# Rebuilding the first ten microseconds of a two-layer encoder kernel on one Trainium2 core

## The chip, the cores and the metric

The kernel runs on one core of a Trainium2 chip. The metric is the device time of one execution in microseconds (us). The kernel before takes 529.43 us, the median of 3 runs (529.13 to 529.46). A profile of one more execution is read as well; that execution took 529.6 us, and its span, from the first to the last instruction, is 527.8 us.

## What is computed

The reference is two layers of a hybrid encoder over 256 tokens of width 1024 in float32. Layer 0 is one shared input projection whose columns feed a Mamba-2 scan (`z`, `xbc`, `dt`) and stick-breaking attention (`q`, `k`, `v`), an output projection, a normalisation, and a mixture of 16 gated experts. Layer 1 has two other kinds of attention and another mixture. Only the very start of layer 0 matters here:

```python
h = x @ w_in
z, xbc, dt_raw, q, k, v = _split(h, [...])        # dt_raw: 16 columns, one per head
...
dt = jax.nn.softplus((dt_raw + dt_bias).astype(f32))
```

## The kernel before

The input is held transposed, `xT`: 128 partitions, 8 chunks of 256 tokens. A product in nearly full float32 precision is made of three cheaper ones: each operand is split into a rounded `hi` part and the remainder `lo`, and `hi*hi`, `hi*lo` and `lo*hi` are accumulated (`mm3_stationary`, L235 to L243). ScalarE writes a `hi` (L231, and L320 for the input), VectorE subtracts to get `lo` (L232, and L321 for the input).

The input projection is cut into 32 strips of 128 columns. Two strips come in one 1 MB weight tile `w`, so strip 0 is the first half of the first tile and strip 1 its second half. A strip costs TensorE 24 products of 128x256 (8 chunks times three parts). `presplit(i)` (L326) emits the split of strip i, two strips ahead of its products. The split parts live in a pool of 3 buffers (`hp`, L101), so the split of strip 3 takes the buffer that strip 0 leaves. Weight tiles come through a ring of 19 buffers that `fill` (L164) keeps full from SyncE's queue (SP in the profile); once the buffers are taken, a load is issued when TensorE or VectorE has finished with an old one.

Each engine works through its own list in the order in which the Python code emits it (a manual schedule); a waiting instruction holds up what is behind it on its engine. The opening, `mixer0` (L306) up to the strip loop (L541), emits in this order:

- SyncE: the 64 KB weights of `dt` (`wdt`, L312), the input in four quarters (L314), then in `load_constants` the first weight tile in two halves, the second tile, the small parameters `pp`, the third tile, the constants `cc` and `cm`, and the rest of the ring.
- ScalarE: the load of an activation table (L248), four pieces of `xh` (L320), the `hi` of strips 0 and 1, a copy of dt's product out of PSUM (L344), the `hi` of strip 2, and so on.
- VectorE: four pieces of `xl` (L321), then the `lo` of strips 0, 1, 2.
- TensorE: dt's product (L340) as plain float32 products, 8 chunks of 128x16 weights by 256 columns, each two records in the trace; then strip 0, strip 1, and so on. Ahead of strip 5, two small transposes (L357) turn dt's product to tokens by heads.

The kernel already has a product of the form that the change gives to dt: the router's logits (L883) put chunk c on the column group c % 4 of TensorE, and one product with the constant `fold` (L893) adds the four groups up.

Of the kernel before, what the change touches and what calls it, by code (L numbers as in the profile page):

```python
# [9 lines left out]
F32 = mybir.dt.float32  # L10
F32R = mybir.dt.float32r
BF16 = mybir.dt.bfloat16
# [81 lines left out]
class Builder:  # L94
# [69 lines left out]
    def fill(self, n=1000, parts=1):  # L164
        while n and self.loaded < len(self.seq) and self.free > self.keep:
            if self.loaded in self.elsewhere:
                self.loaded += 1
                continue
            src = self.seq[self.loaded]
            rows, n_el = src.shape  # L170
            w = self.wp.tile([128, 2048], F32, tag="w", name="w")
            for i in range(parts):
                cs = slice(n_el * i // parts, n_el * (i + 1) // parts)
                self.nc.sync.dma_start(w[:rows, cs], src[:, cs])
            self.ring[self.loaded] = w
            self.loaded += 1
            self.free -= 1
            n -= 1
# [56 lines left out]
    def mm3_stationary(self, ps, hi, lo, xh, xl, n=8):  # L235

        mm = self.nc.tensor.matmul
        for c in range(n):
            mm(ps, hi[:, c, :], xh[:, c, :], start=(c == 0), stop=False)  # L239
        for c in range(n):  # L240
            mm(ps, hi[:, c, :], xl[:, c, :], start=False, stop=False)  # L241
        for c in range(n):
            mm(ps, lo[:, c, :], xh[:, c, :], start=False, stop=(c == n - 1))  # L243


    def load_constants(self):
        nc = self.nc
        nc.scalar.preload_act_table_set(EXP_LN)  # L248
        self.fill(1, 2)
        self.fill(1)  # L250
        self.pp = self.cp.tile([128, NPP], F32, name="pp")
        nc.sync.dma_start(self.pp, self.a["pp"])
        self.fill(1)
        self.cc = self.cp.tile([128, NC0], F32, name="cc")
        nc.sync.dma_start(self.cc, self.a["cc"][:, :NC0])
# [50 lines left out]
    def mixer0(self):  # L306
# [4 lines left out]
        wdt = self.T([128, 8, 16], name="wdt")  # L311
        nc.sync.dma_start(wdt.rearrange("p c n -> p (c n)"), self.a["wdt"])  # L312
        for i in range(4):
            nc.sync.dma_start(xT[:, i * 512:(i + 1) * 512], self.a["xT"][:, i * 512:(i + 1) * 512])  # L314
        self.load_constants()
        xh = self.G([128, 8, 256], F32R, "xh")
        xl = self.G([128, 8, 256], F32R, "xl")
        xT3 = xT.rearrange("p (c t) -> p c t", c=8)
        for i in range(4):
            sc.activation(xh[:, 2 * i:2 * i + 2], xT3[:, 2 * i:2 * i + 2], AF.Copy)  # L320
            v.tensor_sub(xl[:, 2 * i:2 * i + 2], xT3[:, 2 * i:2 * i + 2], xh[:, 2 * i:2 * i + 2].bitcast(F32))  # L321
# [21 lines left out]
        dts = [self.T([128, 512], name="dts")]  # L343
        sc.activation(dts[0][:16, :256], dtp[:16, :256], AF.Copy)  # L344
# [8 lines left out]
        def steps():  # L353
            dtt = self.B("dtt")
            d = dts.pop()
            for t in range(2):
                pe.transpose(dtt[:, 16 * t:16 * t + 16], d[:16, 128 * t:128 * t + 128], self.ident[:16, :16])  # L357
            tmp = self.T([128, 128], name="sptmp")
            v.tensor_add(dt, dtt[:, :32].rearrange("p (t h) -> p t h", t=2),
# [181 lines left out]
        for i in range(32):  # L541
# [1187 lines left out]
def lay_out(inputs):  # L1729
    f = np.ascontiguousarray  # L1730
    x = inputs["x"][0]
    o = {}
# [42 lines left out]
    o["wdt"] = f(dt.reshape(8, 128, 16).transpose(1, 0, 2).reshape(128, 128))  # L1775
# [31 lines left out]
```

## Time and profile before

| | |
|---|---|
| time, median of 3 | 529.43 us (529.13 to 529.46) |
| profiled execution, its span | 529.6 us, 527.8 us |
| TensorE busy | 499.3 us, 95% of the span |
| VectorE, ScalarE, GpSimd busy | 299.5, 247.8, 116.6 us |
| moved from and to memory | 142.37 MB, 270 GB/s over the span |
| first product of TensorE | 4.55 us after the span's start |
| first product of strip 0, of strip 2 | 11.03 us, 16.83 us |

The engines are PE (TensorE; PEld is its weight load, which overlaps products), ACT (ScalarE), DVE (VectorE), POOL (GpSimd) and SP (SyncE); SPq and ACTq are their queues for issuing transfers. All times in rows are counted from the start of the span. A row of the timeline can merge several instructions, and its second number then is the time from the first one's start to the last one's end; a product's end is modelled, so the distance between starts tells more than a length.

### The profile page before, as it was taken

Reading aid. Unit: us, or ns where it says so; the run is one execution under the profiler, and the core shown is the slowest. Engines: PE = TensorE matmul, PEld = TensorE weight load, DVE = VectorE, ACT = ScalarE, POOL = GpSimd, SP = SyncE. Lnnn points to the kernel's source line nnn. Section 1 sums busy time; section 2 is a strip of 40 time slices with the busy share of each in tenths; the row PEclk is TensorE's granted clock in tenths of the full one; section 3 lists DMA queues with packets and bytes.
Section 4 is the critical chain, followed back from the end, with each engine's and each line's share of the span. In section 5 each row is a group of like instructions: output and inputs, shape, how many; then the busy total and the mean of one; then the engine's idle time right before and its main releaser. Section 6 shows DMA issues by size and latency. Waiting matters only on the chain. (4 is left out here: it accounts for less than half of the span.)

```text
span 527.8 us, 9789 instructions
## 1 busy us (share of the span) xinstructions
PE 499.3 (95%) x3844; PEld 321.1 (61%) x3844; DVE 299.5 (57%) x664; ACT 247.8 (47%) x519; POOL 116.6 (22%) x168
## 2 busy tenths in 40 slices
PE   6999999989999999999999998899999999999990
PEld 3999998878677543433323698787777343533320
DVE  3776647678877763160206774788667741512047
ACT  4786565559674442250214683465644431512031
POOL 0073124350300001150002068442000002700204
PEclk9999999999999999999999999999999999999996
DMA  8999942006267969999979923061468799999602
GB/s 281 420 420 417 380 160 81 1 1 240 80 230 266 417 240 395 422 407 418 418 286 418 384 95 138 22 251 69 161 238 329 294 407 409 424 402 425 264 1 79
DMA packets 21178, 142.37 MB, mean 270 GB/s; under 512 B 2372, under 2 KB 2628, under 8 KB 4740
## 3 DMA queue, kind: packets, MB, share of 16 engines
q1 hardware_dynamic: 20024, 135.67, 64.1%
q0 software_dynamic: 816, 5.51, 2.9%
q8 instruction: 32, 0.52, 0.4%
q10 hardware_dynamic: 288, 0.52, 0.3%
q14 instruction: 18, 0.15, 0.1%
HBM read 140.64 MB, written 1.05 MB: 268 GB/s over the span
## 5 line engine op out<-in xcount | busy, mean ns | idle before, releaser
L1022 PE MATMUL gu<-w,XT 128*32 128x512 f32 x960 | 107.0, 593 | 0.0
L232 DVE TENSOR_TENSOR pair<-w,pair 128x1024 fp32r<-128x1024 f32 x50 | 62.7, 1257 | 22.1 <-ACT pair L231 21.8
L1022 PEld LDWEIGHTS gu<-w,XT 128*32 128x32 f32 x960 | 29.7, 110 | 65.4 <-issue 61.5
L231 ACT ACTIVATE pair<-w 128x1024 fp32r<-128x1024 f32 x57 | 60.2, 1059 | 9.1 <-PE ps L243 3.7
L1052 PE MATMUL dn<-w,hT 128*32 128x512 f32 x512 | 59.5, 596 | 0.9 <-ACT hT L1041 0.9
L1032 DVE TENSOR_TENSOR hd<-sg,gu 128x256 f32<-128x256 f32 x16 | 6.7, 421 | 83.5 <-ACT sg L1030 83.4
L779 POOL PARTITION_BROADCAST w<-w x16 | 11.2, 798 | 163.7 <-DMA w<-in_ln_dram 75.9
L1071 DVE SCALAR_TENSOR_TENSOR pair<-dn,ws,pair 128x512 fp32r<-128x512 f32 x30 | 22.5, 749 | 36.4 <-ACT pair L1065 34.4
L239 PE MATMUL ps<-xh,pair 128*128 128x256 f32 x288 | 42.1, 288 | 0.0
L241 PE MATMUL ps<-xl,pair 128*128 128x256 f32 x288 | 39.9, 280 | 0.0
L243 PE MATMUL ps<-xh,pair 128*128 128x256 f32 x288 | 39.8, 280 | 0.0
L1065 ACT ACTIVATE pair<-dn,ws 128x512 fp32r<-128x512 f32 x30 | 20.6, 688 | 37.5 <-PE dn L1052 29.9
L239 PEld LDWEIGHTS ps<-xh,pair 128*128 128x128 f32 x288 | 36.4, 189 | 1.5 <-issue 1.0
L243 PEld LDWEIGHTS ps<-xh,pair 128*128 128x128 f32 x288 | 36.6, 188 | 0.0
L241 PEld LDWEIGHTS ps<-xl,pair 128*128 128x128 f32 x288 | 36.5, 188 | 0.0
L1030 ACT ACTIVATE sg<-gu 128x256 f32<-128x256 f32 x16 | 6.1, 382 | 62.5 <-PE gu L1022 62.5
L1052 PEld LDWEIGHTS dn<-w,hT 128*32 128x32 f32 x512 | 14.4, 109 | 30.7 <-issue 25.7
L992 ACT ACTIVATE XT<-gp,pp 128x256 f32<-128x256 f32 x36 | 17.5, 564 | 19.2 <-PE gp L985 19.2
L232 POOL TENSOR_TENSOR pair<-w,pair 128x1024 fp32r<-128x1024 f32 x7 | 17.0, 2424 | 37.5 <-ACT pair L231 37.5
L1544 ACT ACTIVATE pw<-z,sm 128x128 f32<-128x128 f32 (+1 forms) x32 | 13.0, 420 | 23.4 <-DVE sm L1541 17.0
L394 DVE SCALAR_TENSOR_TENSOR cy<-ps,pp,cy 128x255 f32<-128x255 f32 (+2 forms) x36 | 17.3, 480 | 5.6 <-ACT cy L391 4.8
L302 PE MATMUL vp<-pair,xh 128*128 128x256 f32 x128 | 19.9, 288 | 0.4 <-POOL pair L232 0.4
(371 smaller groups left out, 968.9 us busy)
## 6 DMA issues: line engine op xcount, KB each, us to landing
w<-in_wgu_dram SPq DMA_DIRECT2D x60, 1024.0 KB, 9.8
w<-in_wd_dram SPq DMA_DIRECT2D x32, 1024.0 KB, 11.8
w<-in_w_dram SPq DMA_DIRECT2D x15, 1024.0 KB, 18.1
w<-in_wout_dram SPq DMA_DIRECT2D x10, 1024.0 KB, 18.6
wh<-in_wgu_dram POOLq DMA_DIRECT2D x4, 1024.0 KB, 7.2
w<-in_wfox_dram SPq DMA_DIRECT2D x4, 1024.0 KB, 16.0
w<-in_wfv_dram SPq DMA_DIRECT2D x2, 1024.0 KB, 4.9
w<-in_wab_dram SPq DMA_DIRECT2D x2, 848.0 KB, 17.5
```

The costliest lines, as they stand in the source:

```text
L231: self.nc.scalar.activation(vh, src, AF.Copy)
L232: (self.nc.gpsimd if pool else self.nc.vector).tensor_tensor(vl, src, vh.bitcast(F32), op=OP.subtract)
L239: mm(ps, hi[:, c, :], xh[:, c, :], start=(c == 0), stop=False)
L241: mm(ps, hi[:, c, :], xl[:, c, :], start=False, stop=False)
L243: mm(ps, lo[:, c, :], xh[:, c, :], start=False, stop=(c == n - 1))
L302: mm(o, xx[:, 4 * k + c, 128 * t:128 * t + 128], ww[:, c, :], start=(k == 0 and n == 0), stop=(k == 1 and n == 11))
L394: v.scalar_tensor_tensor(y[:, k:], ps[:, :256 - k], self.pp[:, i:i + 1], y[:, k:], op0=OP.mult, op1=OP.add)
L992: sc.activation(xt[:, c, :], b[:, i], AF.Identity, bias=bb, scale=g)
L1022: pe.matmul(gu[t][32 * e:32 * e + 32, :], XT[t][:, c, o:o + 32], w[:, e, :], start=(c == 0), stop=(c == 7))
L1052: pe.matmul(b[32 * e:32 * e + 32, :], ht[:, k, 32 * e:32 * e + 32], w[:, e, :], start=(k == 0), stop=(k == 1))
L1065: sc.activation(y, dn[t, s], AF.Copy, scale=WS[t][:, q:q + 1])
L1071: v.scalar_tensor_tensor(yl, b, WS[t][:, q:q + 1], yh.bitcast(F32), op0=OP.mult, op1=OP.subtract)
```

## The change

The opening is rebuilt in these parts. The first weight tile is issued from ScalarE's queue, ahead of the table load, in the same two halves; `wdt` is issued from GpSimd's queue and is padded to 32 columns a chunk (128 KB); the input comes in two halves instead of four quarters. VectorE clears a 128x512 bf16 tile, and TensorE multiplies it by itself 8 times into a PSUM buffer that nobody reads. The last two of the four pieces of `xh` move from ScalarE to VectorE. dt's product puts chunk c on column group c % 4, the copy out of PSUM takes 128 partitions instead of 16, and two products with `fold` take the place of the two transposes. Last, strips 0 and 1 both get their `hi*hi` and `hi*lo` products first, and their `lo*hi` products after.

```diff
     def load_constants(self):
         nc = self.nc
+        self.fill(1, 2, nc.scalar)
         nc.scalar.preload_act_table_set(EXP_LN)
-        self.fill(1, 2)
         self.fill(1)
...
-        wdt = self.T([128, 8, 16], name="wdt")
-        nc.sync.dma_start(wdt.rearrange("p c n -> p (c n)"), self.a["wdt"])
-        for i in range(4):
-            nc.sync.dma_start(xT[:, i * 512:(i + 1) * 512], self.a["xT"][:, i * 512:(i + 1) * 512])
+        wdt = self.T([128, 8, 32], name="wdt")
+        nc.gpsimd.dma_start(wdt.rearrange("p c n -> p (c n)"), self.a["wdt"])
+        for cs in (slice(0, 1024), slice(1024, 2048)):
+            nc.sync.dma_start(xT[:, cs], self.a["xT"][:, cs])
         self.load_constants()
+
+        idle = self.T([128, 512], BF16, name="idle")
+        v.memset(idle, 0.0)
+        wu = self.B("wu")
+        for i in range(8):
+            pe.matmul(wu, idle[:, :128], idle, start=True, stop=True)
+        del wu
...
         for i in range(4):
-            sc.activation(xh[:, 2 * i:2 * i + 2], xT3[:, 2 * i:2 * i + 2], AF.Copy)
-            v.tensor_sub(xl[:, 2 * i:2 * i + 2], xT3[:, 2 * i:2 * i + 2], xh[:, 2 * i:2 * i + 2].bitcast(F32))
+            cs = slice(2 * i, 2 * i + 2)
+            if i < 2:
+                sc.activation(xh[:, cs], xT3[:, cs], AF.Copy)
+            else:
+                v.tensor_copy(xh[:, cs], xT3[:, cs])
+            v.tensor_sub(xl[:, cs], xT3[:, cs], xh[:, cs].bitcast(F32))
...
         for c in range(8):
-            pe.matmul(dtp[:16, :256], wdt[:, c, :], xT3[:, c, :], start=(c == 0), stop=(c == 7))
+            r = slice(32 * (c % 4), 32 * (c % 4) + 32)
+            pe.matmul(dtp[r, :256], wdt[:, c, :], xT3[:, c, :], start=(c < 4), stop=(c >= 4))
...
-        sc.activation(dts[0][:16, :256], dtp[:16, :256], AF.Copy)
+        sc.activation(dts[0], dtp[:, :256], AF.Copy)
...
-                pe.transpose(dtt[:, 16 * t:16 * t + 16], d[:16, 128 * t:128 * t + 128], self.ident[:16, :16])
+                pe.matmul(dtt[:, 32 * t:32 * t + 32], d[:, 128 * t:128 * t + 128], self.cv("fold"), start=True, stop=True)
...
+            if i == 0:
+
+                ps2 = [self.A("ps")[:, :256] for _ in range(2)]
+                for k in range(2):
+                    self.mm3_stationary(ps2[k], *pieces[k], xh, xl, parts=(0, 1))
             presplit(i + 2)
             hi, lo = pieces.pop(i)
             ps = None
-            if i >= 28:
+            if i < 2:
+                ps = ps2[i]
+                self.mm3_stationary(ps, hi, lo, xh, xl, parts=(2,))
+            elif i >= 28:
```

In `mm3_stationary`, `parts` chooses among the three loops (0 is `hi*hi`, 1 is `hi*lo`, 2 is `lo*hi`); in `fill`, `queue` names the engine that issues.

## Rows read from the trace of the kernel before

**Rows 1.** The page's first part: busy time, share of the span, instructions of each engine.
```profile
PE 499.3 (95%) x3844; PEld 321.1 (61%) x3844; DVE 299.5 (57%) x664; ACT 247.8 (47%) x519; POOL 116.6 (22%) x168
```

**Rows 2.** PE's waits, whole span: us in total, times, longest us.
```profile
PE dtp L340 <- DMA xT<-in_xT_dram: 4.5, 1, 4.5
PE hT L1462 <- POOL qk L1312: 1.8, 1, 1.8
```

**Rows 3.** Windows: PE, PEld, DVE, ACT, POOL busy (instructions), PEclk, DMA share, GB/s.
```profile
11.00:60.00 49.00, 49.00 (x411) 48.70 (x411) 36.05 (x53) 35.17 (x54) 14.54 (x39) 1.00 1.01 420
60.00:120.00 60.00, 58.34 (x488) 52.82 (x487) 39.15 (x65) 36.21 (x79) 22.86 (x15) 1.00 0.24 88
```

**Rows 4.** Timeline of the opening: start us, us, engine, line, out<-in, count [idle before <-releaser].
```profile
0.81 1.28 ACT L248 ACT_TABLE_LOAD   x1 [0.81 <-PEq L1796]
0.82 0.39 SPq L312 DMA_DIRECT2D wdt<-in_wdt_dram  x1
1.26 1.84 SPq L314 DMA_DIRECT2D xT<-in_xT_dram  x4
3.15 1.38 SPq L174 DMA_DIRECT2D w<-in_w_dram  x3
4.44 0.63 ACT L320 ACTIVATE xh<-xT 128x512 fp32r<-128x512 f32 x1 [2.35 <-DMA xT<-in_xT_dram]
6.68 1.26 ACT L320 ACTIVATE xh<-xT 128x512 fp32r<-128x512 f32 x2 [0.56 <-DMA xT<-in_xT_dram]
9.74 1.06 ACT L231 ACTIVATE pair<-w 128x1024 fp32r<-128x1024 f32 x1 [1.81 <-DMA w<-in_w_dram]
11.02 1.06 ACT L231 ACTIVATE pair<-w 128x1024 fp32r<-128x1024 f32 x1 [0.22 <-DMA w<-in_w_dram]
```

**Rows 5.** Timeline of PE alone, 0 to 17 us.
```profile
4.55 6.55 PE L340 MATMUL dtp<-xT,wdt 128*16 128x256 f32 x16 [4.55 <-DMA xT<-in_xT_dram]
11.03 1.22 PE L239 MATMUL ps<-xh,pair 128*128 128x256 f32 x8
13.98 1.11 PE L239 MATMUL ps<-xh,pair 128*128 128x256 f32 x8
16.83 0.40 PE L239 MATMUL ps<-xh,pair 128*128 128x256 f32 x2
```

**Rows 6.** Windows of the opening, columns as in Rows 3.
```profile
2.00:4.00 2.00, 0.00 (x0) 0.00 (x0) 0.00 (x0) 0.09 (x1) 0.00 (x0) 1.00 0.76 226
4.00:5.00 1.00, 0.45 (x2) 0.20 (x3) 0.00 (x0) 0.56 (x1) 0.00 (x0) 1.00 0.78 238
7.00:8.00 1.00, 1.00 (x4) 0.37 (x3) 0.66 (x2) 0.94 (x2) 0.00 (x0) 1.00 0.95 295
10.00:11.00 1.00, 1.00 (x4) 0.27 (x2) 0.17 (x1) 0.80 (x1) 0.00 (x0) 1.00 1.00 422
```

**Rows 7.** Products of 256 columns, three lines (L239 to 18 us): duration ns min/median/max.
```profile
L340 PE MATMUL dtp<-xT,wdt x16: 379/631/631, 4.5 to 10.7; 128*16 128x256 f32 x16
L428 PE MATMUL cbp<-bc x4: 377/379/381, 34.3 to 38.0; 128*128 128x256 f32 x4
L239 PE MATMUL ps<-xh,pair x24: 277/281/392, 11.0 to 17.7; 128*128 128x256 f32 x24
```

**Rows 8.** Groups by form: busy us, mean ns of one.
```profile
L507 DVE CAST sph<-spz 128x384 fp32r<-128x384 f32 x8 | 2.8, 352 | 0.0
L321 DVE TENSOR_TENSOR xl<-xT,xh 128x512 fp32r<-128x512 f32 x4 | 2.7, 692 | 6.0 <-ACT xh L320 6.0
L232 DVE TENSOR_TENSOR pair<-w,pair 128x1024 fp32r<-128x1024 f32 x50 | 62.7, 1257 | 22.1 <-ACT pair L231 21.8
```

**Rows 9.** Issues from POOL and ACT: duration ns min/median/max, and us to landing of L840's.
```profile
L840 POOL DMA_DIRECT2D wrg<-in_wr_dram x2: 740/801/862, 43.3 to 330.9; - x2
DMA to landing us min/median/max: 2.6/4.6/6.5
...
L799 ACTq DMA_DIRECT2D out_dram<-xres x2: 339/366/394, 522.9 to 524.4; - x2
```

**Rows 10.** Timeline of PE around the router's products in column groups.
```profile
165.90 0.39 PE L684 MATMUL acc<-pair,yh 128*128 128x512 f32 x1
166.22 0.65 PE L883 MATMUL rp<-xT,wrg 128*32 128x128 f32 x16
166.80 0.50 PE L682 MATMUL acc<-pair,yh 128*128 128x512 f32 x1
167.37 0.39 PE L684 MATMUL acc<-pair,yh 128*128 128x512 f32 x1
167.60 0.30 PE L893 MATMUL lg<-cc,rl 128*128 128x32 f32 x2
167.74 0.48 PE L682 MATMUL acc<-pair,yh 128*128 128x512 f32 x1
```

**Rows 11.** Timeline of PE around dt's two transposes.
```profile
25.47 0.29 PE L357 MATMUL dtt<-cc,dts 16*128 16x16 f32 x2
25.69 0.50 PE L239 MATMUL ps<-xh,pair 128*128 128x256 f32 x2
```

**Rows 12.** Timeline of PE, its last products.
```profile
514.14 1.12 PE L1088 MATMUL acc<-yl,PT 128*128 128x512 f32 x2
```

**Rows 13.** Windows after them, columns as in Rows 3.
```profile
517.00:519.00 2.00, 0.00 (x0) 0.00 (x0) 1.93 (x5) 0.66 (x3) 1.92 (x2) 1.00 0.00 0
519.00:520.00 1.00, 0.00 (x0) 0.00 (x0) 0.96 (x2) 0.00 (x0) 1.00 (x2) 0.55 0.00 0
```

More of the change, by code (lines that the diff above doesn't have):

```diff
@@ L162, in load_pair, with fill @@
         self.ring[i] = w
-    def fill(self, n=1000, parts=1):
+    def fill(self, n=1000, parts=1, queue=None):
         while n and self.loaded < len(self.seq) and self.free > self.keep:
@@ L173, in fill @@
                 cs = slice(n_el * i // parts, n_el * (i + 1) // parts)
-                self.nc.sync.dma_start(w[:rows, cs], src[:, cs])
+                (queue or self.nc.sync).dma_start(w[:rows, cs], src[:, cs])
             self.ring[self.loaded] = w
@@ L233, in split, with mm3_stationary @@
         return vh, vl
-    def mm3_stationary(self, ps, hi, lo, xh, xl, n=8):
+    def mm3_stationary(self, ps, hi, lo, xh, xl, n=8, parts=(0, 1, 2)):
         mm = self.nc.tensor.matmul
[L238 to L243, printed above, removed]
+        if 0 in parts:
+            for c in range(n):
+                mm(ps, hi[:, c, :], xh[:, c, :], start=(c == 0), stop=False)
+        if 1 in parts:
+            for c in range(n):
+                mm(ps, hi[:, c, :], xl[:, c, :], start=False, stop=False)
+        if 2 in parts:
+            for c in range(n):
+                mm(ps, lo[:, c, :], xh[:, c, :], start=False, stop=(c == n - 1))
     def load_constants(self):
         nc = self.nc
+        self.fill(1, 2, nc.scalar)
         nc.scalar.preload_act_table_set(EXP_LN)
-        self.fill(1, 2)
         self.fill(1)
@@ L339, in mixer0 @@
         for c in range(8):
-            pe.matmul(dtp[:16, :256], wdt[:, c, :], xT3[:, c, :], start=(c == 0), stop=(c == 7))
+            r = slice(32 * (c % 4), 32 * (c % 4) + 32)
+            pe.matmul(dtp[r, :256], wdt[:, c, :], xT3[:, c, :], start=(c < 4), stop=(c >= 4))
         presplit(0)
         presplit(1)
-        dts = [self.T([128, 512], name="dts")]
-        sc.activation(dts[0][:16, :256], dtp[:16, :256], AF.Copy)
+        dts = [self.T([128, 256], name="dts")]
+        sc.activation(dts[0], dtp[:, :256], AF.Copy)
         del dtp
@@ L356, in steps @@
             for t in range(2):
-                pe.transpose(dtt[:, 16 * t:16 * t + 16], d[:16, 128 * t:128 * t + 128], self.ident[:16, :16])
+                pe.matmul(dtt[:, 32 * t:32 * t + 32], d[:, 128 * t:128 * t + 128], self.cv("fold"), start=True, stop=True)
             tmp = self.T([128, 128], name="sptmp")
-            v.tensor_add(dt, dtt[:, :32].rearrange("p (t h) -> p t h", t=2),
+            v.tensor_add(dt, dtt[:, :64].rearrange("p (t h) -> p t h", t=2)[:, :, :16],
                          self.pv("dtb", 0, 16)[:, None, :].to_broadcast([128, 2, 16]))
@@ L1774, in lay_out @@
     put("rb", np.broadcast_to(rb.reshape(48), (128, 48)))
-    o["wdt"] = f(dt.reshape(8, 128, 16).transpose(1, 0, 2).reshape(128, 128))
+    o["wdt"] = f(np.pad(dt.reshape(8, 128, 16).transpose(1, 0, 2), ((0, 0), (0, 0), (0, 16))).reshape(128, 256))
     wr = np.zeros((2, 1024, 32), np.float32)
```

## The prediction

> **What bounds the kernel now.** First the page's busy shares: PE works in 499.3 of 527.8 us, no other engine over 57% [rows 1]. Then PE's waits: the longest is 4.5 us, at the very start, for the input; the next is 1.8 us, far down, and no later wait on the list is for a weight transfer [rows 2]. Then windows: from 11 to 60 us PE is busy in 49.00 of 49.00 us, and from 60 to 120 us the transfers run at 24% of their engines, because the ring is full [rows 3]. So PE is the bound from strip 0 on, and whatever moves strip 2's first product (16.83 us [rows 5]) moves the end by as much: the weights that the mixtures stream later are issued when PE frees a buffer, so they move along.
>
> The opening itself is read from two timelines. PE waits until 4.55, spends 6.55 us on dt's product, and starts strip 0 at 11.03; strips 0 and 1 then take 16.83 - 11.03 = 5.80 us, 0.121 us a product [rows 5]. Strip 0 has two releasers that come nearly together: dt's product ends, and ScalarE's `hi`, which starts at 9.74 when the first half of the first weight tile has landed, is done at 10.80 [rows 4]. So taking dt's product away alone would give 0.2 us; the transfers have to come sooner too. And dt is slow because PE runs at the lower of its two levels (1.2 GHz, not 2.4): its records are 631 ns long, the last one 379, and the same form later is 377 to 381 [rows 7]. By these lengths the clock rose at about 10.5 us, after some 6.0 us of unbroken work.
>
> **The change part by part.** The sum is made to strip 2's first product, against 16.83.
>
> Transfers. Before, the 64 KB of `wdt` and the 1 MB of `xT` have landed by 7.31 (the third and fourth piece of `xh` run back to back from 6.68), half a tile of weights more by 9.74, the other half by 11.02 [rows 4]: 1.11, 1.64 and 2.16 MB. After, `xT` goes on SP's queue and the weights on ACT's at the same time, `wdt` (twice as large) on POOL's; in all 2.23 MB before strip 1 can be split. The first issue of `xT` moves from 1.26 to 0.82 (0.44 sooner [rows 4]). No row shows three queues starting at once, so T, the landing of the second half of `xT`, is bounded. If it comes after one half of the weights, 1.70 MB, it is the 9.74 of before, plus 0.16 for the larger `wdt` (0.066 MB at 0.42 MB/us [rows 6]), less 0.44: 9.46. If the queues share evenly it comes with the last weights: 11.02 + 0.16 - 0.44 = 10.74. Against that, the transfer engines had room: a share of 0.76 and 226 GB/s at 2 to 4 us, 0.78 and 238 at 4 to 5, 0.95 and 295 at 7 to 8, against 1.00 and 422 at 10 to 11 [rows 6]. Filled up, about 0.3 MB more would have moved, 0.75 us: the range is 8.7 to 10.7. I take 9.6, the even split nearly filled or the other one unfilled. By either, `xT` lands later than the 7.31 of before: that is the price of sending the weights beside it.
>
> The Trainium skill speaks against this part: in "DMA: Bandwidth & Descriptors", section "Issuing engines are not separate DMA queues", it says that transfers issued by several engines run on the same 16 DMA engines, and that a second issuer saves only issue time. The share of 0.76 leaves that open for the start. By the rule T is 9.5 to 10.7, and the change gains at most 0.6 us by the sum below.
>
> First half of `xT`: with half the weights and `wdt` beside it 1.18 MB, so about 7.31 - 0.44 + 0.2 = 7.0. ScalarE's pieces (0.63 each [rows 4]) and VectorE's two subtractions (0.69 each [rows 8]) are done at 7.0 + 0.63 + 1.38 = 9.0. That is before T, but a T under 9.0 would gain nothing more, since VectorE's part below starts then at the earliest.
>
> Products of zeros. PE has nothing until the input lands, so they cost nothing: the clearing (not in the trace; the nearest, VectorE's subtraction over as many columns, is 0.69 [rows 8]) is done by 1.5, 8 products at up to 0.41 each (6.55 / 16, as dt's [rows 5]) end by 4.8, and the input comes at about 7.0. What they may bring is the higher clock by the time of strip 0; see the rivals.
>
> dt's product. Its first half runs before T. The second half, four chunks, is 8 records of 256 columns on four groups: as many columns as the router's 16 of 128, which hold PE from 166.22 to 166.80, drain included [rows 10]. So 0.58 in place of 6.55.
>
> Strip 0. Six of its eight `hi*hi` products run to T + 0.58 + 6 x 0.121 = T + 1.31. The last two need the fourth piece of `xh`, now VectorE's: copy, subtraction, copy. A copy of 384 columns is 352 ns, so 0.47 for 512; with 0.69 between and 0.1 for handing over, T + 1.73 [rows 8]. PE stalls 0.42. Then 42 products remain of 48: 42 x 0.121 = 5.08, and strip 2 starts at T + 6.81. The other inputs come in time: the fourth `xl` at T + 2.4 (needed at T + 2.7), `lo` of strips 0 and 1 at T + 3.7 and T + 4.9 (1.26 each [rows 8]; needed at T + 4.9 and T + 5.9, which is what putting the `lo*hi` parts last buys: in the old order strip 0's would be needed at T + 2.9, a stall of 0.8), and `hi` of strip 1 (1.06) at T + 2.1 if its weights land within 1 us of T (needed at T + 2.9).
>
> With T = 9.6 strip 2 starts at 16.41: a gain of 0.42. Bounds: T = 10.7 gives 17.51, a loss of 0.7; T = 9.0, under which VectorE is late, gives 15.81, a gain of 1.0.
>
> What is moved past what. On ACT's queue two issues (0.37 each [rows 9]) go ahead of the table load, which then ends at 2.85 instead of 2.09, before any input. On SP the second weight tile, `pp` and the rest are issued about 2.4 sooner; the bytes ahead of each are the same, and the second tile, wanted at 16.4, landed at about 13.5 before. On POOL `wdt` has nothing before it; its sister, 128 KB by the same queue, landed 2.6 to 6.5 after its issue of 0.74 to 0.86 [rows 9], so at 4.2 to 8.1. Only dt's first half waits for it, and has until T - 0.58. `hi` of strip 3 waits for strip 0's buffer, which is now released 1.9 later within the pair: it ends 1.06 after T + 5.85, 2.8 before strip 3 starts. The `fold` products cost 0.14 each (167.60 to 167.74 [rows 10]) against 0.22 for both transposes [rows 11]: 0.06, and no change of array shape any more; nothing. The wider copy out of PSUM has the same columns and is not on PE's path.
>
> The sum: 529.6 - 0.42 = 529.2 for an execution like the profiled one. That one was 0.2 over the median, so 529.0.
>
> **Rivals.** *The clock is still low at strip 0.* PE's work comes in three bursts now (zeros to about 4.8, half of dt at 7, the rest from T), and before it needed 6.0 us without a break [rows 5, 7]. For: zeros alone are 3.3 us at most, and at no time before T is there as long a stretch. Against: they use the whole array, dt's 16 columns did not; and pauses of 2 us need not lower a clock that has risen, since at the end it fell only after 519, with PE idle from 515.3 [rows 12, 13]. The Trainium skill, "TensorE: Matmul & The Clock Gate", section "What's actually happening", says that the throttled state is the default and recent activity releases it; by that zeros count like data, but whether 3.3 us of them are enough no row shows. Price: a product at the low level is 631 / 379 = 1.66 times as long, so a microsecond of low clock loses 0.40. If all 6.0 us start again at T: 2.4, plus 0.4 for dt, less the stall of 0.42 that it covers: 2.4. If the earlier bursts count for some of it, about 1.5: 530.5. It decides if more than some 1.2 us of the strips run low.
>
> *The transfers come much better.* If SP's input goes first, landing at about 5.5 and 7.5, and the filled engines bring the first weights by 8.5, `hi` of strip 0 is ready at 9.6, and strips 0 and 1 run without a stall: 9.6 + 5.8 = 15.4, a gain of 1.4: 528.0. For: the share of 0.76. Against: even turns between queues are as likely, and three streams begin together.
>
> *It does nothing:* `xT` and weights land together at 10.5, strip 2 starts at 17.3, and a clock that rises a little sooner in the strips gives nothing back; a loss of 0.5: 529.9. This is the late end of the forecast.
>
> **How the numbers follow.** Forecast (T 9 to 10.7, clock up) 0.47, 528.4 to 530.1 by itself; low clock 0.28; better transfers 0.25. About 0.2% of the time, 1.06 us, is what a measurement of this kernel can tell from no change: same is 528.4 to 530.5. Faster: 0.9 of the third case and 0.15 of the first, 0.30. Slower: 0.8 of the second and a little of the first, 0.23. The range reaches into both rivals, 527.7 to 530.9.
>
> **What would show it.** Right: products of dt on 32 columns about 380 ns long; `xT`'s second half landing later than 7.31; a short stall of PE within strip 0 released by VectorE; strip 2's first product near 16.4; the later windows the same, all shifted by the same amount. Wrong: records of strip 0 longer than the 281 of before [rows 7], which is the clock; strip 0 waiting on ScalarE's `hi` instead of VectorE; a wait for `wdt`; or a shift at 60 us that is gone at the end.

## The result, and the profile after

The changed kernel is slower: 533.51 us (531.13 to 537.05, 7 runs) against 529.46 us (529.09 to 531.26, 7 runs) for the kernel before, a ratio of 1.0073 [1.0056, 1.0090]. Measured again twice, on other occasions, it took 531.45 us (530.67 to 533.38, 12 runs), 1.0028 [1.0009, 1.0047], and 531.53 us (530.99 to 531.80, 7 runs), 1.0029 [1.0017, 1.0040]. So it loses 1.6 to 1.9 us between medians in two series (1.5 by the ratios), and 4 in the first. The forecast of 529.0 was wrong in sign and the time lies outside its range of 527.7 to 530.9; of the rivals the low clock at strip 0, priced at a loss of 1.5 to 2.4, came nearest. Three runs of 630 us and more (two of the kernel without zeros, one of the kernel with dt on column groups alone), all at a mean granted clock under 0.76, are left out of the medians, ranges and ratios below.

The profiled execution is the slowest of the seven, 537.05 us; its span is 535.2 us, 7.4 more than before. The page's first part, to be held against [rows 1]:

```profile
PE 503.5 (94%) x3854; PEld 325.4 (61%) x3854; DVE 303.7 (57%) x667; ACT 246.4 (46%) x517; POOL 117.5 (22%) x169
```

PE is busy for 4.2 us more with 10 more records, though the zeros add only 3.6 and dt's product takes 4.6 less: other products take longer. PE's waits [rows 2] start with another releaser now, and others stand further down (engine, line and tile waited for: us in total, times, longest us):

```profile
PE dtp L355 <- DMA wdt<-in_wdt_dram: 4.7, 1, 4.7
...
PE xp L1315 <- DVE xres L1410: 1.5, 1, 1.5
...
PE gp L1007 <- DVE pair L1094: 0.9, 1, 0.9
...
PE lp L389 <- POOL da L383: 0.4, 1, 0.4
```

The timeline of the opening, all engines, in place of [rows 4, 5]:

```profile
0.81 0.90 ACTq L174 DMA_DIRECT2D w<-in_w_dram  x2
0.82 0.86 SPq L317 DMA_DIRECT2D xT<-in_xT_dram  x2
1.26 3.60 PE L324 MATMUL wu<-idle 128*128 128x512 bf16 x8 [1.26 <-DVE idle L321]
1.32 0.86 POOL L315 DMA_DIRECT2D wdt<-in_wdt_dram  x1 [0.88 <-POOLq L1819]
...
7.22 1.15 ACT L332 ACTIVATE xh<-xT 128x512 fp32r<-128x512 f32 x2 [4.19 <-DMA xT<-in_xT_dram]
...
9.60 1.94 PE L355 MATMUL dtp<-xT,wdt 128*32 128x256 f32 x16 [4.74 <-DMA wdt<-in_wdt_dram]
10.17 0.43 DVE L334 CAST xh<-xT 128x512 fp32r<-128x512 f32 x1 [1.00 <-DMA xT<-in_xT_dram]
...
10.62 1.06 ACT L231 ACTIVATE pair<-w 128x1024 fp32r<-128x1024 f32 x1 [1.31 <-DMA w<-in_w_dram]
...
11.46 2.08 PE L240 MATMUL ps<-xh,pair 128*128 128x256 f32 x8
...
15.04 1.46 PE L240 MATMUL ps<-xh,pair 128*128 128x256 f32 x8
...
19.16 1.10 PE L240 MATMUL ps<-xh,pair 128*128 128x256 f32 x8
```

PE stands still from 4.86 to 9.60 and waits for the 128 KB of `wdt`, though the first half of the input has been there since 7.2. The second half lands at 10.15, the weights of strip 1 at 10.60. Then dt's products and strip 0 run slowly; strip 2 starts at 19.16 instead of 16.83. Two lines by form (duration ns min/median/max) and the issue of `wdt` with its landing, against [rows 7, 9]:

```profile
L355 PE MATMUL dtp<-xT,wdt x16: 634/634/636, 9.6 to 10.9; 128*32 128x256 f32 x16
...
L240 PE MATMUL ps<-xh,pair x16: 277/415/583, 11.5 to 16.2; 128*128 128x256 f32 x16
...
L315 POOL DMA_DIRECT2D wdt<-in_wdt_dram x1: 862/862/862, 1.3 to 1.3; - x1
...
DMA to landing us min/median/max: 8.2/8.2/8.2
```

The windows tell why, with PE, PEld, DVE, ACT and POOL busy, the granted clock, the share of the transfer engines and GB/s, as in [rows 3, 6]; the last four are two stretches far from the change:

```profile
2.00:4.00 2.00, 2.00 (x6) 0.76 (x5) 0.00 (x0) 1.02 (x1) 0.18 (x1) 1.00 0.86 250
4.00:5.00 1.00, 0.86 (x3) 0.00 (x0) 0.00 (x0) 0.00 (x0) 0.00 (x0) 1.00 1.03 262
5.00:9.00 4.00, 0.00 (x0) 0.00 (x0) 1.12 (x2) 1.78 (x3) 0.00 (x0) 1.00 0.98 334
9.00:16.00 7.00, 6.40 (x38) 5.09 (x39) 5.73 (x8) 2.73 (x4) 0.00 (x0) 0.51 1.01 414
...
138.70:142.10 3.40, 2.27 (x21) 1.82 (x22) 2.56 (x13) 0.38 (x1) 1.09 (x2) 1.00 0.63 265
142.10:145.50 3.40, 3.40 (x16) 2.67 (x13) 2.96 (x18) 2.44 (x6) 0.00 (x0) 0.50 0.00 0
340.10:343.50 3.40, 1.71 (x14) 1.28 (x12) 3.40 (x5) 0.38 (x2) 2.93 (x2) 1.00 0.00 0
343.50:346.90 3.40, 3.40 (x17) 3.40 (x17) 2.61 (x6) 1.67 (x9) 0.00 (x0) 0.50 0.00 0
```

The trace's records of the granted clock put its rise at 5.59, just after the zeros end, its fall at 9.0 after 4 us without a product, and its next rise at 15.83: dt's product and the first 4.4 us of strips 0 and 1 run at 1.2 GHz. (A 1.00 ahead of the first such record says nothing: before the change dt's products have 631 ns under it [rows 6, 7].) Then the clock falls twice more in the middle, after stretches in which PE has small products and waits for VectorE and GpSimd. In the profiled execution before, PE is about as little busy there, and the clock stays up:

```profile
135.40:139.00 3.60, 2.45 (x20) 1.73 (x20) 2.76 (x13) 0.38 (x1) 1.40 (x2) 1.00 0.69 271
333.90:337.40 3.50, 1.81 (x16) 1.39 (x15) 3.50 (x5) 0.08 (x1) 2.63 (x2) 1.00 0.00 0
```

How far the same product starts later than before, down the two traces: +0.44 at strip 0, +2.33 at strip 2, +2.8 at 44 us, +3.05 at 63, +4.55 after the first drop, +5.57 at 230, +6.5 at 287, +7.94 at its highest in the second drop, +7.7 at PE's last products. In this one execution 2.3 us are the opening, 0.7 come at 44 to 63 us, where the product `lp` waits for GpSimd's `da`, 2.7 at the two drops (1.5 and 1.2), and 2.0 between the drops, where PE has the waits for `pair` and `xres`; the second is 0.9 longer than before.

### The profile page after: what moved, and what is told of

Same layout as the page of the kernel before. It is cut to its first block, busy times and chain, and to the rows that moved or that the text cites. A ratio compares the mean times of both kernels' runs of the same rounds, so it can differ in the third digit from the quotient of the medians.

```text
span 535.2 us, 9807 instructions
## 1 busy us (share of the span) xinstructions
PE 503.5 (94%) x3854; PEld 325.4 (61%) x3854; DVE 303.7 (57%) x667; ACT 246.4 (46%) x517; POOL 117.5 (22%) x169
## 5 line engine op out<-in xcount | busy, mean ns | idle before, releaser
L240 PE MATMUL ps<-xh,pair 128*128 128x256 f32 x288 | 44.2, 298 | 0.0
L243 PE MATMUL ps<-xl,pair 128*128 128x256 f32 x288 | 41.2, 287 | 0.0
L246 PE MATMUL ps<-xh,pair 128*128 128x256 f32 x288 | 39.6, 280 | 0.0
L240 PEld LDWEIGHTS ps<-xh,pair 128*128 128x128 f32 x288 | 38.4, 199 | 1.8 <-issue 1.8
L243 PEld LDWEIGHTS ps<-xl,pair 128*128 128x128 f32 x288 | 38.0, 196 | 0.0
L246 PEld LDWEIGHTS ps<-xh,pair 128*128 128x128 f32 x288 | 36.4, 188 | 0.0
L1567 ACT ACTIVATE pw<-z,sm 128x128 f32<-128x128 f32 (+1 forms) x32 | 13.0, 419 | 23.7 <-DVE sm L1564 13.1
```

## The experiments

Theory 1: three queues share the transfers, so `wdt`, small and late in the sharing, holds PE in a pause that loses the clock; the cure is PE busy at the higher level until dt. Rival: the price lies in the sharing itself (the input comes 3 us later), or beyond the opening (order, dt's later steps, the drops in the middle). The first six edit one part each, or none.

**`wdt` from SyncE's queue, ahead of the input.** Changed kernel with:

```diff
-        nc.gpsimd.dma_start(wdt.rearrange("p c n -> p (c n)"), self.a["wdt"])
+        nc.sync.dma_start(wdt.rearrange("p c n -> p (c n)"), self.a["wdt"])
```

> The kernel after, with dt's weights issued from SyncE's queue again, ahead of the input. Theory 1 (dt's weights came late from GpSimd's queue: they landed at 9.55 us, PE stood still from 4.86 to 9.60, the clock that the zeros had raised at 5.6 was taken back at 9.0 and strips 0 and 1 ran low until 15.8): the weights land by about 3.5, dt's first half runs at 7.2, the longest pause of PE is about 2.5 us, the clock stays up, strip 2 starts at about 17.0 instead of 19.16, and the time falls by about 2 us, to 531.5. Rival (the price is the input landing at 10.15 instead of 7.3, beside the weights): nothing of this moves the input, so strip 2 starts no sooner than 18.5 and the time stays within 0.7 us of 533.5.

532.35 us (529.76 to 534.77, 12 runs), ratio 1.0038 [1.0018, 1.0058]. PE's timeline:

```profile
8.43 1.08 PE L355 MATMUL dtp<-xT,wdt 128*32 128x256 f32 x8 [3.58 <-DMA xT<-in_xT_dram]
9.92 1.08 PE L355 MATMUL dtp<-xT,wdt 128*32 128x256 f32 x8 [0.41 <-DMA xT<-in_xT_dram]
10.93 2.08 PE L240 MATMUL ps<-xh,pair 128*128 128x256 f32 x8
```

The wait for `wdt` is gone, and the input, behind it, comes 1.1 later (8.3): a pause of 3.6 us remains. In this trace the zeros did not raise the clock at all; it rises only at 13.1. Strip 2 starts at 17.70, 1.5 sooner than in the change's profiled execution and 0.6 to 0.8 sooner than in its two later traces. So the queue of `wdt` by itself doesn't secure the clock. The runs spread over 5 us and their ratio lies between those of the change: a gain in time is not shown.

**Without the zeros.** Changed kernel with:

```diff
-        for i in range(8):
-            pe.matmul(wu, idle[:, :128], idle, start=True, stop=True)
```

(and the lines of `idle` and `wu` around it).

> The kernel after without the eight products of zeros. Theory 1: the clock that they raise is lost again before strip 0, so leaving them out changes nothing that lasts: dt at 9.6, strip 0 at 11.5 at the low level, strip 2 at 19 to 20, the time 533 to 534.5. Rival (the zeros do shorten the low stretch): without them the clock rises later, strip 2 starts at 20.5 or later, and the time is 535 or more.

531.34 us (530.83 to 533.86, 10 runs), 1.0037 [1.0022, 1.0053]. The clock rises at 12.71, strip 0 starts at 11.24, strip 2 at 17.69:

```profile
17.69 1.11 PE L240 MATMUL ps<-xh,pair 128*128 128x256 f32 x8
```

That is 0.6 to 1.5 sooner than in the three traces of the change with them, and sooner than the theory (19 to 20) and the rival (20.5) had it: eight products of zeros buy nothing here.

**26 products of zeros.** Changed kernel with:

```diff
-        for i in range(8):
+        for i in range(26):
```

> The kernel after with 26 products of zeros instead of 8, which keep PE at work until about 9 us. Theory 1: no pause is long enough to lose the clock; dt at 9.6 to 10.9 at the high level, strip 0's records about 281 ns long, strip 2 at about 17.0, the time about 2 us under the kernel after, 531.5. Rival (the late input is the price): strip 2 at 18.5 or later, time within 0.7 us of 533.5.

531.61 us (531.3 to 534.17, 12 runs), 1.0038 [1.0024, 1.0052]. PE's timeline:

```profile
1.26 7.76 PE L324 MATMUL wu<-idle 128*128 128x512 bf16 x26 [1.26 <-DVE idle L321]
...
10.58 1.46 PE L240 MATMUL ps<-xh,pair 128*128 128x256 f32 x8
...
16.58 1.10 PE L240 MATMUL ps<-xh,pair 128*128 128x256 f32 x8
...
489.39 0.47 PE L1113 MATMUL acc<-pair,PT 128*128 128x512 f32 x1 [1.80 <-PEq L1267]
```

The clock rises at 5.29 and stays, and strip 2 starts at 16.58, 0.25 sooner than before the change: the opening goes as theory 1 has it. Only the number of zeros differs from the change, `wdt` still comes late (dt starts at 9.20), and strip 2 starts 1.7 to 2.6 sooner than in the change's three traces: what the opening loses there is the clock. The median does not show it, for PE loses 0.7 by the starts at 44 us and 1.6 more than before at 487 us, behind a branch of its own list (1.80 against 0.18). That wait has come with the added instructions; more of it below. So it is luck that the time is nearly the 531.5 expected: the theory had neither loss.

**Only the first tile moved to ScalarE's queue.** Kernel before with:

```diff
+        self.fill(1, 2, nc.scalar)
         nc.scalar.preload_act_table_set(EXP_LN)
-        self.fill(1, 2)
```

> The kernel before with one part of the change: the first weight tile issued from ScalarE's queue ahead of the table load. Theory 1: the input's last quarter lands at about 9.5 instead of 7.3, dt's product (still 0.43 us a record at the low level) waits for it and ends at about 11.5 to 12, strip 2 starts at 17 to 17.5, and the time is 0.3 to 1.0 us over before: 529.8 to 530.4. Rival (sharing the transfers is the main price): strip 2 starts at 18.5 or later and the time is 531.5 or more.

533.32 us (531.66 to 534.62, 6 runs), 1.0058 [1.0039, 1.0077]. PE's first two lines, and then a window in the middle:

```profile
7.51 5.39 PE L340 MATMUL dtp<-xT,wdt 128*16 128x256 f32 x16 [7.51 <-DMA xT<-in_xT_dram]
12.83 1.22 PE L239 MATMUL ps<-xh,pair 128*128 128x256 f32 x8
```

```profile
140.80:144.30 3.50, 3.50 (x16) 2.78 (x15) 3.07 (x18) 2.39 (x6) 0.00 (x0) 0.51 0.00 0
```

The input lands 3 us later, dt's long product starts 3 us later, and strip 0 1.8. That is more than theory 1 allowed; the rival is nearer here. Sending the weights beside the input has a price of its own here, where dt wants the input first; the short dt of the change makes up for it. One drop in the middle is in this trace too, though it lacks all other parts of the change: of the 3.7 us by which this execution is longer than before, 1.8 come in the opening and 1.5 at the drop.

**The changed kernel again**, unedited.

> The kernel after once more, unchanged, for a second trace and more times. Theory 1 (the loss is made in the opening, by the clock): strip 2 starts 2 to 3 us later than before, records of strips 0 and 1 are 400 ns and more, and the median is 533 to 533.7. Theory 2 (about half of the loss is a second drop of the clock in the middle, at 142 us, which comes by chance in any kernel): the runs fall in two groups about 1.5 us apart, near 531.8 and 533.4.

531.45 us, as above. The clock rises at 4.19, falls at 7.61 and rises at 14.43; strip 2 starts at 18.46 (+1.6), PE waits 0.4 at 44 us, and no drop follows: the profiled execution is 531.71.

```profile
18.46 1.10 PE L240 MATMUL ps<-xh,pair 128*128 128x256 f32 x8
```

The twelve runs lie in three groups by mean granted clock: six at 530.67 to 531.3 (0.989 to 0.993), three at 531.59 to 531.95 (0.984 to 0.987), three at 533.0 to 533.4 (0.980 to 0.983).

**dt on column groups alone.** Kernel before with `wdt` of 32 columns a chunk (still from SyncE), and the copy, the `fold` products and this loop as in the change:

```diff
-            pe.matmul(dtp[:16, :256], wdt[:, c, :], xT3[:, c, :], start=(c == 0), stop=(c == 7))
+            r = slice(32 * (c % 4), 32 * (c % 4) + 32)
+            pe.matmul(dtp[r, :256], wdt[:, c, :], xT3[:, c, :], start=(c < 4), stop=(c >= 4))
```

> The kernel before with one part of the change: dt's product on four column groups, with its wider weights, copy and the two products with fold; weights from SyncE's queue, input in quarters, first tile as before. Theory 1 (dt's long product was also what raised the clock for strip 0): dt is done by about 8.3, PE stands still until 10.9, strips 0 and 1 run at the low level for most of their length, strip 2 starts at 18 to 20 instead of 16.83, and the time is 1.2 to 3 us over before. Rival (a shorter dt is free or gains): strip 2 starts at 16.7 and the time is within 0.3 of before.

531.5 us (530.79 to 532.44, 12 runs), 1.0023 [1.0006, 1.0040]. A part meant to save 6 us of PE makes the kernel slower by itself, by 0.3 to 2.1 us: strip 0 waits for `hi` anyway [rows 4]. That the long dt product had been what raised the clock by 10.52 is theory 1's reading; there is no trace of one of these runs, so here it is argued and not shown.

**`wdt` from SyncE and long zeros.** Changed kernel with `nc.sync` for `wdt` and:

```diff
-        idle = self.T([128, 512], BF16, name="idle")
+        idle = self.T([128, 512], F32, name="idle")
-        for i in range(8):
+        for i in range(4):
```

> The kernel after with dt's weights from SyncE's queue and four plain float32 products of zeros instead of eight bf16 ones: as many instructions on TensorE, but twice as long or more, to about 7 us. Theory 1: PE has no pause over 2.5 us before strip 0, strips 0 and 1 run at the high level in nearly every run, strip 2 starts at 16.4 to 16.9, and the time is 529.3 to 530.2, no better than before because the input and the weights land only at 10.1 to 10.6. Rival (late transfers are the price, not the clock): 531.5 or more.

530.40 us (529.57 to 531.68, 12 runs), 1.0013 [0.9995, 1.0031].

```profile
1.53 5.45 PE L324 MATMUL wu<-idle 128*128 128x512 f32 x8 [1.53 <-DVE idle L321]
8.45 0.64 PE L355 MATMUL dtp<-xT,wdt 128*32 128x256 f32 x8 [1.48 <-DMA xT<-in_xT_dram]
10.09 0.64 PE L355 MATMUL dtp<-xT,wdt 128*32 128x256 f32 x8 [1.00 <-DMA xT<-in_xT_dram]
10.66 1.59 PE L240 MATMUL ps<-xh,pair 128*128 128x256 f32 x8
...
16.78 1.10 PE L240 MATMUL ps<-xh,pair 128*128 128x256 f32 x8
```

As theory 1 says, and with as many PE instructions as the change: zeros of twice the length raise the clock at 5.07, pauses of 1.5 and 1.0 us don't lose it, and the opening's loss, 1.4 to 2.3 us at strip 2 in the three traces of the change, is gone. What is left is 0.7 by the starts at 44 us. The time is a little over the 529.3 to 530.2 expected.

**That, and dt's steps one strip earlier**, ahead of the `fold` products:

```diff
-            if i == 4:
+            if i == 3:
```

> The kernel with dt's weights from SyncE's queue and four float32 products of zeros, and in addition the steps of dt one strip earlier (ahead of strip 4 instead of 5). In that kernel the opening gives 0.1 us back and 0.5 is lost at 44 us, where PE waits for GpSimd's decay (GpSimd's first step of it starts at 28.9 instead of 27.6). Theory: the wait was made by VectorE's later place for dt's addition; one strip earlier it goes away, the shift against before at 60 us is -0.1 to 0.1, and the time falls by 0.4 to 0.6 against that kernel, to about 529.5. Rival: the loss has another place, the shift at 60 us stays over 0.4.

530.35 us (529.13 to 530.98, 12 runs), 1.0001 [0.9988, 1.0013]. The wait at 44 us is gone, and PE runs 0.0 to 0.1 ahead of before at 60 us. It had come from dt's addition on VectorE, which GpSimd's `da` follows: it starts at 27.28 before the change, at 28.62 in the kernel with long zeros, at 26.03 here. By the ratio the time is 0.6 us lower, as expected; the median is hardly lower than the 530.40, with five runs at 529.1 to 529.5 and seven at 530.3 to 531.0. So the change, cured of both, is as fast as before by the ratio, and not faster. Its trace has a drop of the clock from 337.5 to 340.9, which costs 1.2.

**The long zeros with the old order of the `lo` parts**, strips 0 and 1 each whole:

```diff
-            if i == 0:
...
-                    self.mm3_stationary(ps2[k], *pieces[k], xh, xl, parts=(0, 1))
...
-            if i < 2:
-                ps = ps2[i]
-                self.mm3_stationary(ps, hi, lo, xh, xl, parts=(2,))
-            elif i >= 28:
+            if i >= 28:
```

> The kernel with dt's weights from SyncE's queue and four float32 products of zeros, with the products of strips 0 and 1 in the old order (lo*hi of strip 0 before strip 1). Theory: VectorE reaches the lo of strip 0 only about 3.7 us after the input has landed, so PE stalls about 0.8 us before strip 0's last part, strip 2 starts 0.6 to 0.9 later, the time is 0.5 to 0.9 over that kernel, 530.2 to 530.9. Rival: the order is worth nothing, the same start and the same time.

530.35 us (529.95 to 532.03, 12 runs), 1.0008 [0.9994, 1.0021].

```profile
11.59 0.51 PE L240 MATMUL ps<-xh,pair 128*128 128x256 f32 x2 [0.26 <-DVE xh L334]
...
13.45 1.21 PE L246 MATMUL ps<-xh,pair 128*128 128x256 f32 x8 [0.41 <-DVE pair L232]
```

Both stalls that the sum has are there at the higher clock: 0.26 for the fourth `xh` (forecast 0.42) and 0.41 for `lo` in the old order (forecast 0.8). Strip 2 starts at 17.31, against 16.78: putting `lo` last is worth about 0.5 there, and 0.7 counted from the landing of the input's first half, which is 0.16 sooner here. But in the old order dt's addition stands at 27.35 and PE loses nothing at 44 us: at 80 us it is 0.40 behind the kernel before, and 0.59 with `lo` last. The new order has lost by then what it won, and the times (1.0008 against 1.0013) don't tell the two apart.

**Eight products of zeros added to the kernel before**, ahead of the splits of the input:

```diff
+        for i in range(8):
+            pe.matmul(wu, idle[:, :128], idle, start=True, stop=True)
```

> The kernel before with eight bf16 products of zeros ahead of dt and nothing else of the change. Theory 1: they lie ahead of the input and cost nothing; dt follows without a pause over 0.3, the clock rises 0 to 3 us sooner, dt ends at 7.5 to 10 and PE then waits for the weights (10.8), a pause too short to lose the clock; strip 2 at 16.6 to 16.85, time within 0.3 of before. Rival: sixteen more instructions on PE shift its code, and it waits over a microsecond behind the branch at 485 us: 530.5 or more in nearly every run.

530.20 us (529.23 to 531.86, 12 runs), 1.0004 [0.9990, 1.0017]. The clock rises at 6.96, dt's product ends sooner, and strip 0 then waits 1.28 for `hi`; 0.3 us are won in the opening, nothing that the time shows.

**Filling the two stretches in the middle.** The runs of before fall in two groups as well (in one series 8 of 21 have a mean clock of 0.986 to 0.989 and 530.2 to 531.2 us). The drops would explain this. Kernel before with products ahead of the waiting ones, in the router's bias (near 138 us) and in layer 1's attention (near 336 us), at first 24 products of 128 columns:

```diff
+        if layer == 0:
+            for _ in range(10):
+                pe.matmul(rbp[:, 128:256], self.identb, self.onesb, start=True, stop=True)
...
+                if (kind, p, i) == (0, 0, 1):
+                    for _ in range(14):
+                        pe.matmul(b[:, 384:512], self.identb, self.onesb, start=True, stop=True)
```

> The kernel before with products that nobody reads in the two places in the middle where PE waits over 1 us (10 of 128x128 ahead of the router's bias product, 14 ahead of one transpose in the second layer's attention). If the second group of times of the kernel before (530.5 to 531.5, about a third of its runs) is the clock dropping over these places, it goes away: all runs at 529.1 to 529.7. If not, a third of the runs stay at 530.5 or more, and the products may add up to 0.3.

535.9 us (535.07 to 537.0, 6 runs), 1.0109 [1.0078, 1.0139]. PE waits, in the order us in total, times, longest:

```profile
PE gu L1025 <- issue: 2.4, 1, 2.4
PE acc L1093 <- PEq L1247: 2.0, 2, 1.9
```

Both are near 490 us, where nothing was edited, and the clock falls behind them. The question was hidden by a cost of the added instructions. So, the same with three float32 products of 512 columns, two records each:

```diff
+        if layer == 0:
+            pe.matmul(rbp, self.ident, self.cc[:, :512], start=True, stop=True)
...
+                if (kind, p, i) == (0, 0, 1):
+                    for _ in range(2):
+                        pe.matmul(b, self.ident, self.cc[:, :512], start=True, stop=True)
```

> The kernel before with three plain float32 products of 128x512 that nobody reads (12 instructions on PE): one ahead of the router's bias product in layer 0, two ahead of one transpose in layer 1, where PE waits 1.15 and 1.69 us. Theory (the group of runs at 530.4 to 531.3, about two in five, is a drop of the clock over one of these two places): that group goes away, nearly all runs lie at 529.0 to 529.8, none has a granted clock under 0.990. Rival (the drops have another cause): two in five stay at 530.4 or more. If PE's code order matters, all runs move up by over a microsecond, with a wait behind the branch at 485 us.

529.50 us (529.22 to 530.67, 12 runs), against 529.89 of before in the same series (21 runs), 0.9991 [0.9982, 1.0000]. All twelve have a mean clock of at least 0.990. Windows of the two stretches:

```profile
135.40:139.20 3.80, 3.56 (x23) 2.30 (x23) 2.96 (x13) 0.38 (x1) 1.58 (x2) 1.00 0.66 261
334.00:337.50 3.50, 3.50 (x21) 2.24 (x19) 3.50 (x4) 0.88 (x2) 3.41 (x2) 1.00 0.00 0
```

In this series the group of low clock is gone, 0 of 12 runs against 8 of 21, as if the clock dropped in these stretches in some runs of before too; no such run was traced. The slower group is not all clock: three of the twelve still took 530.27 to 530.67, and the profiled one of them (530.55) has no drop. It is 0.2 behind the kernel before from strip 2 on and loses 0.7 more at 229 to 230 us. The same three products in the changed kernel:

> The kernel after with the same three products in the two waits. Theory: the runs at 533 and more (13 of 19 had a granted clock of 0.98 to 0.987) are the opening's low clock and a drop in the middle together; with the drops gone the times lie at 530.7 to 532.2 and none at 533. Rival (533 comes from the opening alone): a third of the runs or more stay at 533.

537.01 us (4 runs), 1.0140 [1.0120, 1.0159]: no drop in the two stretches, but a wait of 2.2 us behind the branch near 490 and a drop after it. The question whether the drops make the runs of 533 us is not answered by it. In the same series the changed kernel ran a third time:

> The kernel after, unchanged, for a third trace. Theory: whatever its time, the shift against before at 44 us is 1 to 3 us by strip 2's start (17.8 to 19.2) and what is above 531.7 in time stands at a drop of the clock in the middle. Rival: a run at 533 with no drop in the middle and an opening that costs 3 us or more.

531.53 us, as above. In its trace the zeros didn't raise the clock at all: it rises at 13.95, strip 2 starts at 18.26, and no drop follows.

```profile
18.26 1.11 PE L240 MATMUL ps<-xh,pair 128*128 128x256 f32 x8
```

The mean clock of this execution reads 0.993 all the same: the time ahead of the first record counts as full in it. So a high mean doesn't say that strips 0 and 1 ran at the higher level.

**The parts that help, on before's transfers.** Kernel before with dt on column groups, two float32 zeros ahead of dt and two behind it, dt's steps at strip 3, and `hi` of strip 0 by two engines:

```diff
-        presplit(0)
+        zeros(2)
...
+        sc.activation(h0[:, :4], w[:, :4], AF.Copy)
+        v.tensor_copy(h0[:, 4:], w[:, 4:])
```

> The transfers as before; dt on four column groups with the clock held up by two float32 products of zeros ahead of it and two behind; hi of strip 0 half by ScalarE and half by VectorE; the steps of dt ahead of strip 4. Theory: PE never pauses over 1.5 us, the first weights land at 9.74 as before, hi of strip 0 is done at 10.35, strip 2 starts at 16.1 to 16.3, no wait at 44 us, and the time is 0.4 to 0.7 under before: 528.8. Rival: what is won in the opening is lost at a later wait, or the clock is low in strip 0 in some runs: 529.4 or more.

529.63 us (528.8 to 530.98, 12 runs), 0.9995 [0.9981, 1.0008]. Strip 2 starts at 15.70, 1.1 sooner than before, and PE keeps that until 336.1, where the clock drops and takes it back. With the three filling products:

> The kernel with the transfers as before, dt on four column groups between products of zeros, hi of strip 0 on two engines and dt's steps ahead of strip 4, and with the three products in the two waits. Theory: its runs without a drop lay at 528.8 to 529.5, those with one at 530 to 531; with the drops gone nearly all lie at 528.4 to 529.3, 0.1 to 0.2% under before's median. Rival: some other wait, or the place of PE's code, takes it back: 529.5 or more.

533.67 us (5 runs), 1.0073 [1.0060, 1.0086]. The gain of 0.9 lasts to 485 us; then:

```profile
486.00:488.70 2.70, 0.34 (x4) 0.00 (x0) 0.92 (x2) 0.69 (x1) 0.00 (x0) 1.00 1.01 410
488.70:492.10 3.40, 3.33 (x8) 2.48 (x8) 0.00 (x0) 0.00 (x0) 0.00 (x0) 0.50 1.02 417
```

**With fewer instructions.** dt as before, two float32 zeros, the split `hi`, the steps at strip 3, the three filling products: 10 more PE records than before, as the change has.

> The kernel before with what the runs so far point to, in 20 more instructions on PE (as many as the kernel after): two float32 products of zeros ahead of dt, dt's product as before, hi of strip 0 half by ScalarE and half by VectorE, dt's steps ahead of strip 4, and the three products in the two waits in the middle. Transfers as before. Theory: PE is at work from 1.5 us to strip 0 without a pause over 1 us, the clock rises by 8.1, strip 0 starts at 10.0 to 10.4 and strip 2 at 15.8 to 16.2, no drop in the middle, no wait behind the branch; nearly all runs at 528.3 to 529.2, 0.15 to 0.25% under before's median. Rival: the code's place costs again, as in the kernels with 32 more (533), or a wait at 230 or 287 us takes the gain: 529.5 or more.

529.28 us (528.74 to 530.83, 12 runs), against 529.77 (17 runs), 0.9991 [0.9979, 1.0004].

```profile
1.53 3.67 PE L320 MATMUL wu<-idle 128*128 128x512 f32 x4 [1.53 <-DVE idle L317]
5.13 3.63 PE L345 MATMUL dtp<-xT,wdt 128*16 128x256 f32 x16
10.14 1.22 PE L239 MATMUL ps<-xh,pair 128*128 128x256 f32 x8 [1.38 <-ACT pair L348]
...
15.94 1.11 PE L239 MATMUL ps<-xh,pair 128*128 128x256 f32 x8
```

Strip 2 starts 0.9 sooner and the trace keeps it to the end (span 527.0). Two of the twelve runs, at 530.8, have a mean clock of 0.988 although the two stretches are filled; they were not traced. The interval takes in 1, so a version that beats the kernel before is not shown. PE still waits 1.38 for the first weights there: what is left of the opening is the transfers.

## Why the prediction was wrong

- **The step that failed:** the sum takes the clock to be up from T on: 0.58 for dt's second half and 0.121 a product in strips 0 and 1. Behind it stood `wdt` at 4.2 to 8.1, and so a pause of some 2 us after the zeros. `wdt` landed at 9.55, 8.2 us after its issue. "Only dt's first half waits for it, and has until T - 0.58" held even so (9.57 with the T measured); the harm was in the pause. PE stood still for 4.7 us, the clock that the zeros had raised fell at 9.0, dt's records took 634 ns, and strips 0 and 1 took 7.70 us instead of the 6.23 of the sum. The bounds for `wdt` came from a sister transfer [rows 9]: 2.6 us at 331 us, where the transfer engines had a share of 0.23 at most, and 6.5 at 43 us, where they were full (1.00 to 1.06). Neither had two other queues starting beside it.
- **The rival "the clock is still low at strip 0"** is what happened; it had a chance of 0.28. The zeros do count: with 26 of them, or four of twice the length, the clock rose at 5.1 to 6.5 us, before PE had done anything else. This agrees with the Trainium skill ("TensorE: Matmul & The Clock Gate", section "What's actually happening"), by which the throttled state is the default and activity releases it. But three traces of the change have it rise at 5.59, at 4.19 and not before dt, and in the first two the pause undid it. My "against" was that a pause of 2 us need not lower the clock; that held (1.5 us did not), but the pause was 4.7. The price: with T = 10.15, strip 0 should have started at 10.73 and strip 2 at 16.96. Strip 0 started 0.73 later (dt slow, and its first half just ahead of the second), and strips 0 and 1 took 1.47 longer: 2.20 in all, near the upper price of 2.4. In the two later traces, with T at 10.05 and 10.00, it is 1.60 and 1.45, as the middle price.
- **T:** 10.15 measured, in the range of 8.7 to 10.7, but not the 9.6 taken: another 0.55 of loss at strip 2. The weights landed 0.45 behind it: the queues shared almost evenly. The step "filled up, about 0.3 MB more would have moved" was wrong: at 2 to 4 us the share rose from 0.76 to 0.86 and the rate only from 226 to 250 GB/s; at 4 to 5 us a share of 1.03 goes with 262. A busy share below one was not room for 420 GB/s here. The rule of the Trainium skill that the prediction weighed ("DMA: Bandwidth & Descriptors", section "Issuing engines are not separate DMA queues") had it right: transfers issued by several engines run on the same DMA engines. The trace agrees with it: T is within the 9.5 to 10.7 worked out by it, and the last weights land at 10.60, where even sharing gave 10.74.
- **The first half of the input:** 7.2 against 7.0. Right.
- **dt's second half at 0.58:** right at the higher level (10.09 to 10.66 with the long zeros), 1.3 at the lower one. **VectorE's piece:** copies of 0.43 and a stall of 0.26 against 0.42. **`lo` last:** 0.5 to 0.7 against 0.8, and lost again at 44 us. The forecast's own case can be seen with the clock held: strip 2 at 16.78, where T + 6.81 gives 16.9 with T = 10.09.
- **`fold` costing nothing:** nearly right on PE (0.36 to the next product, against 0.22). But the sum left out that with `lo` last VectorE comes to dt's addition 1.3 us later, at the same start of strip 2 (28.62 against 27.28; 31.00 in the change, where the opening's loss adds to it), and that GpSimd and PE wait behind it: 0.5 to 0.7 by the starts at 44 us in every trace of the change, gone with the steps one strip earlier and with the old order.
- **Zeros costing nothing:** right; what they bring by themselves is nothing the time shows (1.0004 on the kernel before).
- **"The later windows the same, all shifted by the same amount":** wrong. In two stretches, in which PE is busy for half to two thirds of the time, the clock can fall, at 1.5 and 1.2 us in the profiled execution. By the mean clocks this happens in runs of before as well, and none of the twelve runs with the stretches filled shows it.

Not settled: why five of seven runs of the first series took 533 us and the later series mostly 531. Only the one trace at 537 has both drops; the traces at 531.6 and 531.7 have none; no run of the change at 533 was traced, and in the kernel that was to tell, the wait near 490 hides it. That the drops make that group is argued from the mean clocks (0.980 to 0.983), not shown.

## What to carry to other kernels

A free queue did not bring the small transfer sooner here: the 128 KB of `wdt` landed 8.2 us after their issue on a queue of their own beside 2 MB, and 4.3 us after it at the head of the input's queue. What that costs the transfers behind it has to be set against it. Before shortening an engine's work in an opening, ask whether that work is what raises its clock, and leave no long pause between a warm-up and the first real product. Where gains of under 1 us are sought, look at the mean clock of every run first: two groups of runs can hide or feign such a gain. And follow a part beyond the place where it gains: `lo` last won 0.5 at strip 2 and lost it at 44 us.

## What the runs showed that was not expected

The clock can fall in the middle of a dense kernel: after some microseconds in which PE was busy for half to two thirds of the time with small products, it ran at 1.2 GHz from 142.1 to 145.5 and from 343.5 to 346.9, at a price of 1.5 and 1.2 us, in some executions and not in others of the same program. Four traces of other kernels have one such drop each, at 140.8 or at 336 to 338 us.

Added PE instructions can cost time far away. In every trace with up to 10 more PE records than before the wait behind the branch near 487 us is the usual 0.2; in all four with 16 (the two filled kernels that build on the change or on its parts), 24 (24 fillers) or 28 (26 zeros) more it is 1.8 to 2.4. Where the code lies in memory is a guess at the cause; no run here tests it.
